# The modulation product of a decoder layer, feature tile by feature tile over four column groups

## The chip, the core and the metric

The kernel runs on one core of one Trainium2 chip. TensorE multiplies matrices into PSUM, VectorE (DVE), ScalarE (ACT) and GpSimd (POOL) work on rows of 128 partitions, and SyncE (SP) issues most of the DMAs. The engines run side by side, each its own instructions in a fixed order, and meet through semaphores. The metric is the device time in microseconds of one execution; of several runs the median counts.

## The reference

One decoder layer works on 1024 prompt tokens and on 8 sample sequences of 4 new tokens each, all of width 1024. Nine modulation vectors for each of nine conditions (the prompt's and eight samples') shift, scale and gate its three parts:

```python
mods = (silu(cond) @ ada_w + ada_b).reshape(B, 9, 1, 1024)
h = rms_norm(x, norm_ffn1) * (1 + mods[:, 1]) + mods[:, 0]
x = x + 0.5 * mods[:, 2] * swiglu_ffn(h, ffn1_wi, ffn1_wo)
h = rms_norm(x, norm_mix) * (1 + mods[:, 4]) + mods[:, 3]
...
x = x + mods[:, 5] * mix
h = rms_norm(x, norm_ffn2) * (1 + mods[:, 7]) + mods[:, 6]
x = x + 0.5 * mods[:, 8] * swiglu_ffn(h, ffn2_wi, ffn2_wo)
```

`mix` comes from a gated delta rule and from latent attention over a cache. `ada_w` is 1024 x 9216 in float32, 37.7 MB. The product with it has nine rows only, so nearly all of its work is to bring these weights past the array.

## The kernel before

The residual stream lies with features on partitions: three blocks (`xb`) of 352 token columns (1056 in all), each with 8 feature tiles of 128. The program is: load and transpose x, first norm, first FFN, mixer, second FFN. The order on each engine is set when the program is built, by a scheduler that simulates it; a few stretches of POOL are ordered by hand. On the chip every engine keeps that order.

**The modulation product** is the generator `ada(m0, nm, ...)` (L215). It makes `nm` vectors from number `m0` on, 1024 outputs each, cut into slices of 512. The conditions after silu (`cT`, padded to 32 columns, one tile per feature tile) are the stationary operand, the weights stream. Slice j accumulates in partitions 32j to 32j+31 of one PSUM bank (`acc`), which are columns 32j to 32j+31 of the array, a column group. The loops run slice by slice: for each j four loads (L225) of 256 features x 512 outputs (512 KB), and behind each load its two matmuls (L227) of 128 features; then a `yield`. So all eight feature tiles of one slice come before the next slice begins. At the end the rows are copied (`adarow`, L232), transposed (`adaT`, L235), and added to the bias (L239) into `modT`.

- Vectors 0 and 1 are made in the start (L1944), between the sums of the first norm and its application, with seven buffers of their own (`adaw` in the pool t0).
- Vector 2 alone, then 3 and 4, 5 and 6, 7 and 8 are made in the background of the first FFN (`background`, L1949). Their loads pass through the three buffers `wraw`, which the FFN's weights use too. The FFN calls `hook(us)` with a rough measure of the work done (L1959); for each PACE (1.85 for vector 2, then 8.0) the background goes on by one step, a load and its two matmuls.

**The FFN** (`ffn`, L345) takes 44 tiles of hidden features, two at a time. `up` makes gate and up products (`pg`), `down` the product with the second weights (`po`). Every weight tile is loaded into `wraw` (L106, L111), split by ACT (L97) and POOL or DVE (L100) into two float32r parts `whi` and `wlo`, and each product is three matmuls (`mm3`, L116 to L118) over 352 columns.

**SyncE** issues all these loads in one queue, in order: a load that waits for its buffer holds back what stands behind it.

Of the kernel before, what the change touches and what calls it, by code (L numbers as in the profile page):

```python
# [8 lines left out]
F32 = mybir.dt.float32  # L9
# [8 lines left out]
P = 128  # L18
# [16 lines left out]
# the projections of the mixer in turn: keys, queries, values and gates of GDN, latents and queries of MLA; from I on the  # L35
# triangular systems, from F on the norms of MLA's queries run beside
# [27 lines left out]
PACE = (1.85, 8.0)  # L64
# [6 lines left out]
class Banks:  # L71
    """PSUM pools by tag"""
# [8 lines left out]
class Kernel:  # L81
# [21 lines left out]
    def load_cols(self, w, c0, n):  # L103
        """n columns of w [1024, *] as a [128, 8, n] tile pair"""
        raw = self.wraw.tile([P, KT, P], F32, tag="wraw", name="wraw")
        self.nc.sync.dma_start(out=raw[:, :, :n], in_=w[:, c0:c0 + n].rearrange("(k p) c -> p k c", p=P))  # L106
        return raw
# [26 lines left out]
    def weights(self):  # L134
        """the pools that weights pass through, as a context"""
# [5 lines left out]
    def residents(self):  # L141
        """the residual stream, as a context"""
# [5 lines left out]
    def r(self, tp, shape, name, dt=F32):  # L148
        """a tile of the mixer's shared 1152-word slots"""
        return tp.tile(shape, dt, tag="r", name=name, bufs=RBUFS)  # L150

    def segs(self, c0, n):
        """token columns c0..c0+n as (block, column in block, length, offset)"""
# [8 lines left out]
    def tok_tiles(self):  # L162
        """(block, column, tokens, [(row, tokens, prompt?, first token)]) of the nine token tiles that no block edge cuts"""
# [11 lines left out]
    def load_x(self, ps, tag):  # L175
        """the residual stream, feature on the partition; the rows pass through the tiles of the first norm's results"""
# [16 lines left out]
    def small_vectors(self, tp, ps, tag):  # L193
        """ada_b (72 rows of 128) and the three norm gains (8 each), feature on the partition"""
# [20 lines left out]
    def ada(self, m0, nm, tp, ps, tag, bufs=0):  # L215
        """nm (1 or 2) modulation vectors from m0 on: silu(c) @ ada_w + ada_b, transposed; yields between loads"""
# [3 lines left out]
        for j in range(2 * nm):  # L220
            c0 = m0 * D + j * 512
            for kp in range(4):
                raw = (tp.tile([P, 2, 512], F32, tag="adaw", name="adaw", bufs=bufs) if bufs
                       else self.wraw.tile([P, 2, 512], F32, tag="wraw", name="adaw"))
                nc.sync.dma_start(out=raw, in_=w[kp * 256:(kp + 1) * 256, c0:c0 + 512].rearrange("(k p) c -> p k c", p=P))  # L225
                for k in range(2):
                    nc.tensor.matmul(acc[32 * j:32 * j + 32, :], self.cT[:, 2 * kp + k, :], raw[:, k, :],  # L227
                                     start=(kp == 0 and k == 0), stop=(kp == 3 and k == 1))
                yield
        row = tp.tile([P, 512], F32, tag="adarow", name="adarow", bufs=1)  # L230
        np_ = 64 * nm
        nc.scalar.copy(row[:np_], acc[:np_])  # L232
        pt = ps.tile([P, 4, 4, 32], F32, tag=tag, name="adaT")
        for q in range(4):
            nc.tensor.transpose(pt[:, q, :2 * nm, :].rearrange("p j r -> p (j r)"), row[:np_, q * P:(q + 1) * P], self.ident[:np_, :np_])  # L235
        bias = self.vecs[:, 0:72].rearrange("p (m k) -> p m k", k=KT)
        for j in range(2 * nm):
            m, k0 = m0 + j // 2, (j % 2) * 4
            nc.vector.tensor_tensor(out=self.modT[:, m, k0:k0 + 4, :], in0=pt[:, :, j, 0:NROW],  # L239
                                    in1=bias[:, m, k0:k0 + 4].unsqueeze(2).to_broadcast([P, 4, NROW]), op=ALU.add)  # L240
# [4 lines left out]
    def mod_finish(self, m):  # L245
        """scale rows become g * (1 + scale); the FFN gates are halved"""
# [9 lines left out]
    def norm(self, mscale, mshift, tp, ps, between=None):  # L256
        """between() is called where its work comes before the last of the norm's"""
# [8 lines left out]
    def norm_squares(self, b, tp, k=0, n=KT, eng=None):  # L266
        """the squares of features k..k+n of block b, added up"""
# [15 lines left out]
    def norm_sums(self, blocks, tp, ps):  # L283
        """the inverse roots of some blocks, a quarter of a block per column"""
# [13 lines left out]
    def norm_apply(self, b, mscale, mshift, tp, ps, turn=0):  # L298
        """the parts of block b, the first in the place of block b + turn"""
# [31 lines left out]
    def residual(self, b, d, m, ps, tp):  # L331
        """x += gate * ps for feature tile d of token block b"""
# [12 lines left out]
    def ffn(self, wi, wo, mgate, tp, ps, each, hook=lambda us: None, banks="B"):  # L345
        """each(b, d) follows when feature tile d of block b is complete"""
# [5 lines left out]
        def up(ffs):  # L352
            """some tiles of the hidden features, block by block"""
# [35 lines left out]
        for c in chunks:  # L389
            # the first tiles go together, as the norm of the later blocks is not there yet  # L390
# [10 lines left out]
    def store_y(self, ps, tag, block, halves):  # L401
        """the results of a block, or of halves of its features"""
# [52 lines left out]
    def proj_weights(self, eng=None):  # L455
        """the next tile of w_in's columns in the order of self.worder, as (hi, lo, columns)"""
# [15 lines left out]
    def proj(self, evac, ps, post=None):  # L472
        """the next tile of w_in's columns, transposed: evac(b, psum, rows); what follows from earlier tiles goes between its
# [1451 lines left out]
def body(tc, ins, outs):  # L1925
    k = Kernel(tc, ins, outs)
    nc = tc.nc
    with k.ctx:
        k.setup()
        k.dram()  # L1930
        def run(gen):
            for _ in gen:
                pass
# [87 lines left out]
```

## Time and profile before

| what | us |
| --- | --- |
| median of 3 runs (2957.89 to 2968.86) | 2967.14 |
| profiled execution, first to last instruction (span) | 2962.4 |
| start, up to the first matmul of the first FFN | 59.4 |
| first FFN, up to the mixer's first projection | 59.4 to 942.3 |
| mixer up to its output projection | 942.3 to 2087.9 |
| TensorE busy | 2824.4 |

For the profiled execution only the span is given; what lies around it is not shown apart.

How to read the profile: PE is TensorE's matmuls, PEld its weight loads, which overlap with them. A row of the timeline gives start, length, engine, line, operation, written tile <- read tiles, shape and count; rows of one kind that follow each other are merged, and the length reaches to the end of the last one, whose end is modelled. "[idle <-X]" is the time for which the engine stood still before, and what ended it. A matmul in float32 shows as two records. L12 is line 12 of the kernel; the lines of the changed kernel are shifted by a few.

### The profile page before, as it was taken

How to read it: one execution, taken by the hardware profiler on the slowest of the kernel's cores; microseconds unless marked ns; L12 is line 12 of the kernel's file. 1: busy time of each engine (PE TensorE's matmuls, PEld its weight loads, DVE VectorE, ACT ScalarE, POOL GpSimd, SP SyncE). 2: the span in 40 equal slices, each digit the busy share in tenths (PEclk: the TensorE clock that was granted, in tenths of full speed). 3: DMA queues.
4: the chain of work that ended last, by engine and by line, in shares of the span. 5: the costliest groups of instructions: out<-in, count | busy, mean ns of one | idle time of the engine just before them, and what ended most of it. 6: DMA issues, size and time to landing. Idle time of an engine off the chain costs nothing.

```text
span 2962.4 us, 45680 instructions
## 1 busy us (share of the span) xinstructions
PE 2824.4 (95%) x18596; PEld 2548.1 (86%) x18596; DVE 1579.8 (53%) x3258; ACT 919.0 (31%) x1674; POOL 801.9 (27%) x624
## 2 busy tenths in 40 slices
PE   7999999999998989889999988898899999999999
PEld 4788888899998889778887866675899999999998
DVE  5232322233337568997777677886463343333445
ACT  4211111111113453433676664443341111111111
POOL 3100011111113344445344456452221111111110
PEclk8999999999999999999999998997899999999999
DMA  7322233221113257344122234322301111111111
GB/s 234 108 86 79 86 100 93 76 67 43 43 39 101 69 159 194 121 142 148 33 58 60 58 68 129 87 62 48 120 29 58 43 50 51 43 43 44 57 36 59
DMA packets 295385, 238.76 MB, mean 81 GB/s; under 512 B 89390, under 2 KB 248870, under 8 KB 294408
## 3 DMA queue, kind: packets, MB, share of 16 engines
q1 hardware_dynamic: 285624, 207.54, 24.0%
q0 software_dynamic: 6144, 20.98, 2.2%
q10 hardware_dynamic: 3408, 7.33, 0.8%
q8 instruction: 146, 2.39, 0.3%
q14 instruction: 63, 0.52, 0.1%
HBM read 192.66 MB, written 43.15 MB: 80 GB/s over the span
## 4 chain that ended last, share of the span: by engine, by line
PE 41%; DVE 8%; issue 5%; POOL 4%; DMA 1%; ACT 1%; POOLq 0%; DVEq 0%; ACTq 0%
PE pg L116 6%; PE pg L118 6%; PE pg L117 6%; PE po L116 4%; PE po L117 4%; PE po L118 4%; POOL gt L1344 2%; PE kraw L116 1%; PE kraw L118 1%; PE kraw L117 1%; POOL gS L1344 1%; DVE cy L708 1%; DVE kss L1820 1%; PE pS L116 1%; DVE pv L522 1%
## 5 line engine op out<-in xcount | busy, mean ns | idle before, releaser
L116 PE MATMUL pg<-hhi,whi 128*128 128x352 f32 x2112 | 685.9, 325 | 1.9 <-ACT hhi L324 1.9
L118 PE MATMUL pg<-hhi,wlo 128*128 128x352 f32 x2112 | 680.9, 323 | 0.0
L117 PE MATMUL pg<-hlo,whi 128*128 128x352 f32 x2112 | 679.7, 322 | 0.5 <-POOL hlo L325 0.5
L336 DVE SCALAR_TENSOR_TENSOR x<-po,modT,x 128x352 f32<-128x352 f32 (+1 forms) x552 | 313.8, 572 | 573.3 <-PE po L118 566.1
L100 POOL TENSOR_TENSOR wlo<-wraw,whi 128x1024 fp32r<-128x1024 f32 x93 | 225.7, 2432 | 1422.7 <-ACT whi L97 1372.4
L116 PEld LDWEIGHTS pg<-hhi,whi 128*128 128x128 f32 x2112 | 396.9, 188 | 27.2 <-issue 18.4
L117 PEld LDWEIGHTS pg<-hlo,whi 128*128 128x128 f32 x2112 | 399.2, 189 | 3.3 <-issue 1.7
L118 PEld LDWEIGHTS pg<-hhi,wlo 128*128 128x128 f32 x2112 | 396.7, 188 | 5.9 <-issue 5.9
L116 PE MATMUL po<-ahl,whi 128*128 128x352 f32 x1056 | 344.2, 326 | 2.6 <-DVE rt L340 1.3
L117 PE MATMUL po<-ahl,whi 128*128 128x352 f32 x1056 | 339.9, 322 | 0.0
L118 PE MATMUL po<-ahl,wlo 128*128 128x352 f32 x1056 | 338.8, 321 | 0.0
L97 ACT CAST whi<-wraw 128x1024 fp32r<-128x1024 f32 x140 | 145.6, 1049 | 541.7 <-PE po L117 231.9
L366 DVE TENSOR_TENSOR fa<-fs,pg 128x352 f32<-128x352 f32 x132 | 68.4, 518 | 368.7 <-ACT fs L364 368.6
L364 ACT ACTIVATE fs<-pg 128x352 f32<-128x352 f32 x132 | 61.1, 463 | 581.4 <-PE pg L118 581.4
L1820 DVE TENSOR_REDUCE kss<-ksq 128x8 f32<-128x512 f32 x256 | 173.6, 681 | 80.5 <-ACT ksq L1819 78.3
L116 PEld LDWEIGHTS po<-ahl,whi 128*128 128x128 f32 x1056 | 198.0, 188 | 13.2 <-issue 8.9
L1819 ACT ACTIVATE ksq<-kraw 128x512 f32<-128x512 f32 x256 | 152.7, 599 | 156.7 <-PE kraw L118 120.5
L117 PEld LDWEIGHTS po<-ahl,whi 128*128 128x128 f32 x1056 | 200.0, 189 | 0.0
L118 PEld LDWEIGHTS po<-ahl,wlo 128*128 128x128 f32 x1056 | 198.5, 188 | 0.0
L116 PE MATMUL pp<-hhi,whi 128*128 128x352 f32 (+1 forms) x576 | 191.2, 333 | 5.7 <-ACT raw L689 2.4
L118 PE MATMUL pp<-hhi,wlo 128*128 128x352 f32 (+1 forms) x576 | 192.0, 335 | 2.9 <-POOL tss L719 2.1
L117 PE MATMUL pp<-hlo,whi 128*128 128x352 f32 (+1 forms) x576 | 190.6, 331 | 3.0 <-DVE hlo L328 2.0
(490 smaller groups left out, 4973.3 us busy)
## 6 DMA issues: line engine op xcount, KB each, us to landing
wraw<-ffn_wi SPq DMA_DIRECT2D x88, 512.0 KB
adaw<-ada_w SPq DMA_DIRECT2D x72, 512.0 KB
wraw<-ffn_wo SPq DMA_DIRECT2D x44, 512.0 KB
wraw<-w_in SPq DMA_DIRECT2D x23, 512.0 KB
x_d<-x SPq DMA_DIRECT2D x3, 1408.0 KB
x<-x_d SPq DMA_DIRECT2D x3, 1408.0 KB
dml<-dm_d SPq DMA_DIRECT2D x8, 512.0 KB
wraw<-w_out SPq DMA_DIRECT2D x8, 512.0 KB
```

The source lines that it names most:

```text
L97: nc.scalar.copy(hi, raw)
L100: eng.tensor_tensor(out=lo, in0=raw, in1=f(hi), op=ALU.subtract)
L116: nc.tensor.matmul(out, whi, ahi, start=first, stop=False)
L117: nc.tensor.matmul(out, whi, alo, start=False, stop=False)
L118: nc.tensor.matmul(out, wlo, ahi, start=False, stop=last)
L336: nc.vector.scalar_tensor_tensor(out=x[:, d, :n], in0=ps[:, :n], scalar=self.modT[:, m, d, 0:1], in1=x[:, d, :n], op0=ALU.mult, op1=ALU.add)
L364: nc.scalar.activation(s, pg[:, 0, :BW], AF.Silu)
L366: nc.vector.tensor_tensor(out=a, in0=s, in1=pg[:, 1, :BW], op=ALU.mult)
L522: nc.vector.tensor_tensor(out=t, in0=y, in1=y, op=ALU.mult)
L1344: mul = lambda out, a, b, op=ALU.mult: nc.gpsimd.tensor_tensor(out=out, in0=a, in1=b, op=op)
L1819: nc.scalar.activation(sq, kr, AF.Square)
L1820: nc.vector.tensor_reduce(out=ss[:, (j * 4 + m) * H:(j * 4 + m + 1) * H], in_=sq.rearrange("p (h d) -> p h d", h=H), axis=AX.X, op=ALU.add)
```

## The change

The four slices of two vectors (or of one vector, see below) advance together. A step loads two pieces of 128 features x 1024 outputs, 512 KB each, and issues four matmuls, one for each column group. For two vectors (`nm` = 2) the pieces are the same feature tile of both vectors, and there are eight steps. For one vector they are feature tiles s and s + 4 of that vector: column groups 0 and 1 sum up the first four feature tiles, groups 2 and 3 the last four, there are four steps, and the second pair of rows is added to the first after the transposes. `issue_after` puts the matmuls of groups 3, 0 and 1 behind that of group 2 on TensorE.

In the FFN the first piece of a step still goes through `wraw`; the second has one buffer of its own (`adaw`, bufs 1, in the pool tk). PACE is doubled, as a step now does the work of two. The rest of the diff takes out comments, and shifts the lines below.

```diff
--- before
+++ after
-PACE = (1.85, 8.0)
+PACE = (3.7, 16.0)
...
     def ada(self, m0, nm, tp, ps, tag, bufs=0):
...
         acc = ps.tile([P, 512], F32, tag=tag, name="ada")
-        for j in range(2 * nm):
-            c0 = m0 * D + j * 512
-            for kp in range(4):
-                raw = (tp.tile([P, 2, 512], F32, tag="adaw", name="adaw", bufs=bufs) if bufs
-                       else self.wraw.tile([P, 2, 512], F32, tag="wraw", name="adaw"))
-                nc.sync.dma_start(out=raw, in_=w[kp * 256:(kp + 1) * 256, c0:c0 + 512].rearrange("(k p) c -> p k c", p=P))
-                for k in range(2):
-                    nc.tensor.matmul(acc[32 * j:32 * j + 32, :], self.cT[:, 2 * kp + k, :], raw[:, k, :],
-                                     start=(kp == 0 and k == 0), stop=(kp == 3 and k == 1))
-                yield
+
+        def load(n, k, c0):
+            raw = (tp.tile([P, 1024], F32, tag="adaw", name="adaw", bufs=bufs or 1) if bufs or n
+                   else self.wraw.tile([P, 1024], F32, tag="wraw", name="adaw"))
+            nc.sync.dma_start(out=raw, in_=w[k * P:(k + 1) * P, c0:c0 + 1024])
+            return raw
+        nk = KT // (3 - nm)
+        for s in range(nk):
+            ks = (s, s) if nm == 2 else (s, s + nk)
+            raws = [load(n, k, m0 * D + (n * 1024 if nm == 2 else 0)) for n, k in enumerate(ks)]
+            def product(j):
+                return nc.tensor.matmul(acc[32 * j:32 * j + 32, :], self.cT[:, ks[j // 2], :], raws[j // 2][:, (j % 2) * 512:(j % 2) * 512 + 512],
+                                        start=(s == 0), stop=(s == nk - 1))
+
+            with self.tc.issue_after(product(2).ins):
+                for j in (3, 0, 1):
+                    product(j)
+            yield
         row = tp.tile([P, 512], F32, tag="adarow", name="adarow", bufs=1)
-        np_ = 64 * nm
-        nc.scalar.copy(row[:np_], acc[:np_])
+        nc.scalar.copy(row, acc)
         pt = ps.tile([P, 4, 4, 32], F32, tag=tag, name="adaT")
         for q in range(4):
-            nc.tensor.transpose(pt[:, q, :2 * nm, :].rearrange("p j r -> p (j r)"), row[:np_, q * P:(q + 1) * P], self.ident[:np_, :np_])
+            nc.tensor.transpose(pt[:, q].rearrange("p j r -> p (j r)"), row[:, q * P:(q + 1) * P], self.ident)
         bias = self.vecs[:, 0:72].rearrange("p (m k) -> p m k", k=KT)
-        for j in range(2 * nm):
-            m, k0 = m0 + j // 2, (j % 2) * 4
-            nc.vector.tensor_tensor(out=self.modT[:, m, k0:k0 + 4, :], in0=pt[:, :, j, 0:NROW],
-                                    in1=bias[:, m, k0:k0 + 4].unsqueeze(2).to_broadcast([P, 4, NROW]), op=ALU.add)
+        for j in range(4):
+            m, k0 = m0 + (j // 2 if nm == 2 else 0), (j % 2) * 4
+            v = self.modT[:, m, k0:k0 + 4, :]
+            nc.vector.tensor_tensor(out=v, in0=pt[:, :, j, 0:NROW],
+                                    in1=bias[:, m, k0:k0 + 4].unsqueeze(2).to_broadcast([P, 4, NROW]) if nm == 2 or j < 2 else v, op=ALU.add)
```

More of the change, by code (lines that the diff above doesn't have):

```diff
@@ L1943, in modulation @@
                             k.key_tables(tp, ps, "C")
-                            run(k.ada(0, 2, tp, ps, "C", 7))
+                            run(k.ada(0, 2, tp, ps, "C", 6))
                         k.load_x(ps, "C")
```

## The prediction, made before the changed kernel ran

> **What bounds the kernel now.** I read the page first, then the stages, then every place where L227, the modulation product, stands on TensorE. The page's line of busy times and its 40 slices say that TensorE is the bound except at the very start and in parts of the middle.
>
> ```profile
> PE 2824.4 (95%) x18596; PEld 2548.1 (86%) x18596; DVE 1579.8 (53%) x3258; ACT 919.0 (31%) x1674; POOL 801.9 (27%) x624
> PE   7999999999998989889999988898899999999999
> ```
>
> The second view gives busy time by stretch (start:end, length, then for each engine busy us and instructions; behind them the granted TensorE clock, the DMA share and GB/s). The rows are the first FFN with the background beside it (60 to 713 holds all of L227 that is left after the start), the stretch in which the mixer's work is mixed (1070 to 2088), and the second FFN.
>
> ```profile
> 60.00:713.00 653.00, 652.48 (x3597) 561.63 (x3597) 205.18 (x437) 109.43 (x179) 84.50 (x42) 0.99 0.27 81
> 1070.00:2088.00 1018.00, 916.42 (x7258) 771.90 (x7256) 787.27 (x1619) 510.19 (x1006) 474.64 (x433) 0.94 0.36 99
> 2185.00:2962.40 777.40, 770.61 (x4844) 767.52 (x4842) 334.40 (x657) 144.25 (x232) 110.09 (x51) 1.00 0.15 48
> ```
>
> In the first FFN TensorE idles 0.5 us of 653, the clock is full, and no other engine is busy for a third of the time. What is taken from TensorE there comes off the end one for one. The second FFN is the same work without a modulation product beside it: 777 us with TensorE still 99% busy, so the other engines keep that pace. The first takes 942.3 - 59.4 = 883, by the timeline's rows for its first matmul and the mixer's:
>
> ```profile
> 59.42 0.59 PE L116 MATMUL pg<-hhi,whi 128*128 128x352 f32 x2 [1.87 <-ACT hhi L324]
> ...
> 942.28 0.52 PE L116 MATMUL pp<-hhi,whi 128*48 128x352 f32 x2 [0.91 <-ACT hhi L324]
> ```
>
> The view by stretch for L227 alone shows what stands to be taken:
>
> ```profile
> 28.00:60.00 32.00, 25.05 (x64) 6.05 (x64) 0.93 0.80 262
> 60.00:713.00 653.00, 103.61 (x224) 20.24 (x224) 0.99 0.27 81
> ```
>
> The 288 records are 144 matmuls, so each float32 matmul leaves two. 64 records stand in the start, 224 in the FFN.
>
> **The FFN's part, before.** The timeline (start, length with the last one's tail, line, count) around one visit of the product among the FFN's matmuls, and around two longer visits:
>
> ```profile
> 112.37 0.32 PE L118 MATMUL pg<-hhi,wlo 128*128 128x352 f32 x1
> 112.63 1.90 PE L227 MATMUL ada<-adaw,cT 128*32 128x512 f32 x4
> 114.46 0.43 PE L116 MATMUL pg<-hhi,whi 128*128 128x352 f32 x1
> 114.73 0.32 PE L117 MATMUL pg<-hlo,whi 128*128 128x352 f32 x1
> 114.89 0.32 PE L118 MATMUL pg<-hhi,wlo 128*128 128x352 f32 x1
> ...
> 162.94 3.65 PE L227 MATMUL ada<-adaw,cT 128*32 128x512 f32 x12
> ...
> 330.14 5.34 PE L227 MATMUL ada<-adaw,cT 128*32 128x512 f32 x12
> ```
>
> Matmuls of the FFN start 0.16 us apart (114.73, 114.89). From the start at 112.37 to that at 114.73 there are 2.36 us where two steps of 0.16 would do: the visit costs 2.04 us. In the run at 330.14 twelve records start within 5.34 less one tail of 0.59, so they are (5.34 - 0.59) / 11 = 0.43 us apart. Four of those are 1.72; the other 0.32 us is what going to the narrow shape and back costs (0.31 with unrounded starts). Between these two rows the timeline has 49 visits:
>
> ```profile
> 68.02 1.04 PE L227 MATMUL ada<-adaw,cT 128*32 128x512 f32 x2
> ...
> 596.88 1.90 PE L227 MATMUL ada<-adaw,cT 128*32 128x512 f32 x4
> ```
>
> 224 x 0.43 + 49 x 0.31 = 111.5 us. The run at 162.94 is 1.69 us shorter than its twin at 330.14, which is four records: there the end of one slice met the start of the next, in another column group, and their records ran side by side. That makes 109.8 us, and the two FFNs differ by 883 - 777 = 106.
>
> **Four side by side.** The trace has one line that already feeds four column groups in turn, the product of exponentials and latents (L1702, float32, 32 output rows each, 128 columns wide):
>
> ```profile
> 1737.34 1.95 PE L1702 MATMUL psc<-ck,pr 128*32 128x128 f32 x64
> ```
>
> By width one such record takes 0.43 / 4 = 0.107 us. One after the other 64 would take 6.9 us; four at a time they take 16 x 0.107 = 1.7 plus a tail, and 1.95 is what stands there. So four groups run at four times the rate, with four different moving operands. That a 512 wide product does the same is seen for two groups only (162.94).
>
> The order on TensorE at one visit in the first FFN (adaw is a loaded piece of the weights, ada the accumulator; each row x2 is two matmuls), before:
>
> ```order
> L118 MATMUL po_1210<-ahl_740,wlo_1199 128x352
> L227 MATMUL ada_786<-adaw_1218,cT_64 32x512 x2
> L227 MATMUL ada_786<-adaw_1294,cT_64 32x512 x2
> L227 MATMUL ada_786<-adaw_1382,cT_64 32x512 x2
> L116 MATMUL po_1222<-ahl_668,whi_1192 128x352
> ```
>
> and at the corresponding place of the changed kernel:
>
> ```order
> L118 MATMUL po_1212<-ahl_740,wlo_1201 128x352
> L232 MATMUL ada_819<-adaw_1238,cT_64 32x512 x2
> L232 MATMUL ada_819<-adaw_1236,cT_64 32x512 x2
> L116 MATMUL pg_1448<-hhi0_442,whi_1438 128x352
> ```
>
> The two rows of the changed kernel are the four column groups of one step. Counted through its whole order, the 28 steps in the first FFN make 33 visits: 24 whole, and four steps torn into two or three pieces. A visit then costs two records after each other, 0.86, some 0.02 for starts that are not quite together, and 0.31 for the change of shape: 1.19 us, whether it holds one matmul or four. 33 x 1.19 = 39.3. **The FFN gains 109.8 - 39.3 = 70.5 us.** Bounds from the nearest rows: only two at a time, as at 162.94, gives 28 x 4 x 0.43 + 33 x 0.31 = 58.4 and a gain of 51; the change of shape at nothing gives 28 x 0.88 and a gain of 85. I take 70.5, for L1702 shows both the four and the same change of shape.
>
> The Trainium skill, page "TensorE: Matmul & The Clock Gate", section "Measured speedup vs the span model", states 2.38 times for three column tiles of 512 and 3.07 times for four row tiles, less than the trace's four. By 3.07 a whole step would take 8 x 0.43 / 3.07 = 1.12 instead of 0.88 us, and the gain would be 28 x 0.24 = 6.7 us less; no row here shows four groups at 512.
>
> **The start.** There 25.05 us of product stand between the first norm's sums and its end, on the path:
>
> ```profile
> 28.34 9.17 PE L227 MATMUL ada<-adaw,cT 128*32 128x512 f32 x20 [0.34 <-DVE idx L437]
> 38.78 7.08 PE L227 MATMUL ada<-adaw,cT 128*32 128x512 f32 x20
> 46.24 8.80 PE L227 MATMUL ada<-adaw,cT 128*32 128x512 f32 x24
> 55.72 0.66 PE L235 MATMUL adaT<-ident,adarow 128*128 128x128 f32 x4 [0.68 <-ACT adarow L232]
> ```
>
> Eight steps of 0.88 would be 7 us, 18 less, but the weights are not there so soon:
>
> ```profile
> 32.00:36.00 4.00, 4.00 (x10) 0.91 (x10) 2.23 (x4) 2.23 (x3) 1.69 (x1) 0.93 0.90 241
> 48.00:52.00 4.00, 4.00 (x15) 1.18 (x14) 0.00 (x0) 0.00 (x0) 0.00 (x0) 1.00 1.05 388
> 52.00:56.00 4.00, 3.32 (x11) 0.83 (x9) 0.00 (x0) 0.90 (x2) 0.00 (x0) 1.00 0.20 74
> 56.00:60.00 4.00, 1.75 (x14) 1.15 (x12) 3.43 (x11) 3.26 (x7) 0.56 (x1) 0.98 0.02 3
> 60.00:64.00 4.00, 3.48 (x13) 3.46 (x13) 4.00 (x7) 3.36 (x8) 3.19 (x4) 0.50 0.00 0
> ```
>
> The DMA runs at its full share up to 52 us plus 4 x 74 / 388 = 0.8. The queue of SyncE before, behind the fourth FFN weight (wraw_597):
>
> ```order
> L225 DMA adaw_397<-ada_w 128x2x512
> L225 DMA adaw_632<-ada_w 128x2x512
> L225 DMA adaw_401<-ada_w 128x2x512
> L225 DMA adaw_405<-ada_w 128x2x512
> L225 DMA adaw_409<-ada_w 128x2x512
> L225 DMA adaw_413<-ada_w 128x2x512
> L225 DMA adaw_417<-ada_w 128x2x512
> L225 DMA adaw_421<-ada_w 128x2x512
> L225 DMA adaw_636<-ada_w 128x2x512
> L225 DMA adaw_671<-ada_w 128x2x512
> ```
>
> and now, behind the same weight (632, 671 and 704 belong to the next vector):
>
> ```order
> L225 DMA adaw_403<-ada_w 128x1024
> L225 DMA adaw_632<-ada_w 128x1024
> L225 DMA adaw_409<-ada_w 128x1024
> L225 DMA adaw_671<-ada_w 128x1024
> L225 DMA adaw_411<-ada_w 128x1024
> L225 DMA adaw_417<-ada_w 128x1024
> L225 DMA adaw_419<-ada_w 128x1024
> L225 DMA adaw_704<-ada_w 128x1024
> ```
>
> Before, two foreign loads followed the last own one, 0.52 MB each, 1.35 us at 388 GB/s: the last own one (421) landed near 52.8 - 2.7 = 50.1, and TensorE was done with it at 55.0. Now two foreign loads stand ahead of the last own one (419) instead of one: 1.35 us later, less about 0.5 for the pause at 32 to 36 (share 0.90), which earlier freed buffers fill: about 51.0. One step more, 0.9 to 1.7 us by clock, ends at 51.9 to 52.7. **The start gains 2.7 us**, its cover being the DMA; bounds 0 and 18. The Trainium skill, the page named above, section "What's actually happening", has the array fall to half its clock after an idle window of some 3.4 us; the row at 60 to 64 (0.50 behind a stretch with 1.75 of 4 us busy) agrees, and by it the last step takes the 1.7. What follows, norm and first FFN matmuls, moves up unchanged; it ran at half clock at 60 to 64 already.
>
> **Costed at nothing.** Two more adds on VectorE, a 128 row copy on ScalarE and full transposes for the one vector alone lie beside TensorE's work in the FFN. DMA volume is the same. The order in the mixer between 1070 and 2088 comes out differently, with the same instructions: nothing on average, though TensorE idles 102 us there and its clock is 0.94, so a reshuffle has room both ways; I allow 15 us, an estimate: a tenth of that idle time and lost clock (0.06 x 1018 = 61).
>
> **Sum.** 70.5 + 2.7 = 73.2. The span would fall from 2962.4 to 2889.2. The median of the runs shown is 2967.1, 4.7 above the span; less 73.2 it is **2894 us**.
>
> **Rivals.** (a) Two at a time: as above the FFN gains 51, the start 2: 2914. Speaks for it: at 512 wide the trace shows two only. Against: L1702.
> (b) The four do not overlap at all: 28 x 8 x 0.43 + 33 x 0.31 = 106.6 against 109.8, and no gain at the start: 2964. Both rows above speak against it.
> (c) The mixer's new order costs or gives over 20 us: 2915 to 2945, or under 2872.
> (d) Slower: each step's second piece has a single buffer, so its load is issued only when the step before is through, and SyncE's FFN weights wait behind it. A load on idle queues:
>
> ```profile
> 71.23 2.72 SPq L225 DMA_DIRECT2D adaw<-ada_w  x2
> ...
> 72.00:73.00 1.00, 1.00 (x5) 0.43 (x4) 1.00 (x3) 0.97 (x3) 0.42 (x1) 1.00 0.72 78
> 73.00:74.00 1.00, 1.00 (x5) 0.52 (x4) 1.00 (x3) 0.84 (x2) 0.64 (x1) 1.00 0.90 338
> 74.00:75.00 1.00, 1.00 (x8) 1.00 (x7) 1.00 (x3) 0.75 (x2) 0.50 (x1) 1.00 0.65 139
> ```
>
> Issued at 71.23, its 0.52 MB are through near 74.5: 3.3 us. Were it exposed at all 28 steps, it would cost 92 us: 2986. It decides from 73.2 / 28 = 2.6 us of wait per step. Against it: the closest steps in the new order have 30 matmuls between them, 30 x 0.16 = 4.8 us, which leaves 1.5 to spare; it would take other waits in SyncE's queue ahead of the load.
>
> **Chances and range.** The forecast (2872 to 2913) 0.78; (c) 0.05 up and 0.05 down; (a) 0.05; (b) 0.03; (d) 0.04. The range 2872 to 2916 takes in the forecast, (a) and the mixer's 15 us. Faster by over 0.5% (15 us, about what a measurement of this kernel can tell from no change): 0.93; within: 0.03; slower: 0.04.
>
> **What would show it.** The product's busy time in the first FFN falls from 103.6 to about 35 us; its visits read x8 and last about 1.1 us; the mixer's first projection starts some 73 us earlier. Two at a time would read 1.9 us per x8. In the start TensorE waits for adaw, and its last product ends near 52. Rival (d) shows as waits of TensorE for adaw or whi beyond 60 us. A mixer stretch longer or shorter than 1018 us by over 15 makes the sum wrong.

## The result and the profile after

The changed kernel takes **2893.0 us** (median of 5 runs, 2880.28 to 2896.78) where the kernel before takes 2967.14 (2957.89 to 2968.86, now of 5 runs): a ratio of 0.975, 95% interval 0.9726 to 0.9774, so 74.1 us less, where 73.2 were predicted. Two more measurements of the same changed kernel follow among the experiments: 2900.46 and 2894.56.

The profiled execution was the fastest of the five (2880.28, span 2878.3). Its page's busy line and the slices of TensorE and of its clock:

```profile
PE 2745.4 (95%) x18596; PEld 2527.9 (88%) x18596; DVE 1586.6 (55%) x3260; ACT 916.9 (32%) x1674; POOL 803.8 (28%) x624
...
PE   6999999999999898889999988888999999999999
...
PEclk7999999999999999989999999997999999999999
```

TensorE has the same 18596 instructions and is busy 79 us less. The view by stretch shows where: the first FFN with the background beside it, the whole first FFN, the mixed part of the mixer (up to its output projection), the second FFN; then the modulation product's line (now L232) alone, in the start and in the first FFN.

```profile
60.00:713.00 653.00, 653.00 (x4054) 618.01 (x4053) 237.26 (x497) 122.69 (x200) 93.69 (x45) 1.00 0.28 85
57.90:868.40 810.50, 807.13 (x5001) 769.28 (x5001) 308.92 (x658) 156.53 (x251) 126.91 (x67) 1.00 0.27 81
996.80:2005.40 1008.60, 918.50 (x7257) 770.36 (x7255) 785.06 (x1618) 508.10 (x1003) 475.51 (x433) 0.94 0.35 99
2101.70:2878.30 776.60, 769.78 (x4841) 766.61 (x4839) 334.12 (x657) 144.19 (x232) 109.60 (x51) 1.00 0.15 48
```

```profile
28.00:60.00 32.00, 13.89 (x64) 1.60 (x60) 0.55 0.77 267
60.00:713.00 653.00, 35.04 (x224) 5.07 (x224) 1.00 0.28 85
```

In the window from 60 to 713 us TensorE is busy all 653 us, and more FFN matmuls fit into it (4054 records, 3597 before). The product's own time there fell from 103.61 to 35.04 us. The first FFN took 883 us and takes 810.4; the second is unchanged (777). One visit of the product on TensorE's timeline:

```profile
276.55 0.32 PE L118 MATMUL pg<-hhi,wlo 128*128 128x352 f32 x1
276.80 1.07 PE L232 MATMUL ada<-adaw,cT 128*32 128x512 f32 x8
277.80 0.43 PE L116 MATMUL pg<-hhi,whi 128*128 128x352 f32 x1
278.06 0.32 PE L117 MATMUL pg<-hlo,whi 128*128 128x352 f32 x1
```

Eight records end within 1.07 us; from the FFN's last start before them (276.55) to the second behind them (278.06) are 1.51 us, less two steps of 0.16 that would stand there anyway: 1.19 us for a visit. The first FFN has 33 visits, and none of them has idle time before it. Its first two:

```profile
64.80 1.06 PE L232 MATMUL ada<-adaw,cT 128*32 128x512 f32 x6
66.95 1.05 PE L232 MATMUL ada<-adaw,cT 128*32 128x512 f32 x2
```

They are one torn step: two records cost a visit (1.17 us) as much as eight (1.19).

One line of the change is missing from the diff shown above: in the start, `run(k.ada(0, 2, tp, ps, "C", 7))` became `run(k.ada(0, 2, tp, ps, "C", 6))`, so six buffers hold the start's loads instead of seven. The seventh load therefore waits for the first step, which an experiment below takes up.

### The profile page after: what moved, and what is told of

Same layout as the page of the kernel before. It is cut to its first block, busy times and chain, and to the rows that moved or that the text cites. A ratio compares the mean times of both kernels' runs of the same rounds, so it can differ in the third digit from the quotient of the medians.

```text
span 2878.3 us, 45708 instructions
## 1 busy us (share of the span) xinstructions
PE 2745.4 (95%) x18596; PEld 2527.9 (88%) x18596; DVE 1586.6 (55%) x3260; ACT 916.9 (32%) x1674; POOL 803.8 (28%) x624
## 4 chain that ended last, share of the span: by engine, by line
PE 43%; DVE 7%; issue 5%; POOL 4%; DMA 2%; ACT 1%; POOLq 0%; DVEq 0%; ACTq 0%; SPq 0%
PE pg L116 6%; PE pg L118 6%; PE pg L117 6%; PE po L116 4%; PE po L117 4%; PE po L118 4%; POOL gt L1353 2%; PE kraw L116 1%; PE kraw L118 1%; PE kraw L117 1%; POOL gS L1353 1%; PE pS L116 1%; DVE kss L1829 1%; PE pS L117 1%; PE pS L118 1%
```

## Experiments

Each edit is against the changed kernel. Stage lengths are read from TensorE's timeline: the first FFN runs from its first matmul to the mixer's first projection.

### One column group at a time

The change's steps, two loads and four matmuls each, and its turns; but the four matmuls of a step are four feature tiles of one slice, in one column group. With that the loads have the old shape again (256 features x 512 outputs, still 512 KB), and the copies and transposes at the end are the old ones.

```diff
-            nc.sync.dma_start(out=raw, in_=w[k * P:(k + 1) * P, c0:c0 + 1024])
+            nc.sync.dma_start(out=raw.rearrange("p (k c) -> p k c", k=2), in_=w[k * 256:(k + 1) * 256, c0:c0 + 512].rearrange("(k p) c -> p k c", p=P))
...
-        nk = KT // (3 - nm)
-        for s in range(nk):
-            ks = (s, s) if nm == 2 else (s, s + nk)
+        steps = [(j, kq) for j in range(2 * nm) for kq in range(2)]
+        for j, kq in steps:
...
-                return nc.tensor.matmul(acc[32 * j:32 * j + 32, :], self.cT[:, ks[j // 2], :], raws[j // 2][:, (j % 2) * 512:(j % 2) * 512 + 512],
+                return nc.tensor.matmul(acc[32 * j:32 * j + 32, :], self.cT[:, 4 * kq + k, :], raws[k // 2][:, (k % 2) * 512:(k % 2) * 512 + 512],
```

> Undoes the column groups alone: the step of the change (two loads, four matmuls, doubled PACE, the second load's own buffer) stays, but the four matmuls of a step belong to one slice and so to one column group, slice by slice as before. The order has 35 visits in the first FFN. Theory (side by side is what counts): 224 records at 0.43 us and 35 visits at 0.31 us, 107 us on top of the FFN's own work of 771 us (810.4 less 33 x 1.19): the first FFN takes 878 us, the kernel 2960 us, within 0.5% of before. Rival (fewer and longer visits or the loads' shape are what counts): the first FFN stays near 810 us, the kernel near 2893.

Measured: 2969.86 us, ratio 0.9991 (0.9973 to 1.0008). A whole step on the timeline:

```profile
123.16 0.32 PE L118 MATMUL pg<-hhi,wlo 128*128 128x352 f32 x1
123.42 3.62 PE L233 MATMUL ada<-adaw,cT 128*32 128x512 f32 x8
126.97 0.43 PE L116 MATMUL pg<-hhi,whi 128*128 128x352 f32 x1
...
62.20:936.10 873.90, 97.63 (x224) 20.70 (x224) 2.34 (x4) 1.00 0.25 75
```

The last row is the product's line over the first FFN. The same eight records that take 1.07 us side by side take 3.62 us in one column group. Fewer and longer visits gave 9 us in the first FFN (873.9 against 882.9), some of it where the end of one slice met the next; the other 63.5 us of the gain come with the column groups. This kernel undoes the loads' shape as well, so it does not part the two; the next one does, for it keeps the new loads.

### Two column groups at a time

One load and the two matmuls that read it make a step, and PACE is the old one.

```diff
-PACE = (3.7, 16.0)
+PACE = (1.85, 8.0)
...
-        for s in range(nk):
-            ks = (s, s) if nm == 2 else (s, s + nk)
-            raws = [load(n, k, m0 * D + (n * 1024 if nm == 2 else 0)) for n, k in enumerate(ks)]
+        for s, n in ((s, n) for s in range(nk) for n in range(2)):
+            k = s if nm == 2 else s + n * nk
+            raw = load(0, k, m0 * D + (n * 1024 if nm == 2 else 0))
...
-            with self.tc.issue_after(product(2).ins):
-                for j in (3, 0, 1):
-                    product(j)
+            with self.tc.issue_after(product(2 * n).ins):
+                product(2 * n + 1)
```

> Two column groups at a time: a step is one load of 128 features x 1024 outputs and its two matmuls, with the PACE of before and all loads of the FFN through wraw. 48 visits in the first FFN, between one and six matmuls each. Theory: a visit costs 0.31 us and every round of records 0.43 us, some 110 to 120 rounds: 62 to 67 us on top of 771, a first FFN of 833 to 838 us and a kernel of 2916 to 2921 us. Rival (the gain is not the rounds but the number of visits, 49 before, 48 here, 33 in the change): the first FFN near 880 us and the kernel near 2965.

Measured: 2922.1 us, ratio 0.982 (0.9788 to 0.9852), and a first FFN of 835.8 us. A step (first row), and the product's line over the first FFN:

```profile
103.10 1.05 PE L233 MATMUL ada<-adaw,cT 128*32 128x512 f32 x4
...
57.90:893.70 835.80, 54.77 (x224) 8.14 (x224) 2.35 (x4) 1.00 0.26 79
```

Two groups side by side take as long (1.05 us) as four do (1.07), and as one matmul alone does: the price belongs to the visit. The total lies 1 us above the range expected, the first FFN inside it. Here are 48 visits (43 of about 1.18 us, five with three steps and 2.03 us), 61.0 us in all where the change's 33 cost 39.3, and the first FFN is 25 us longer.

### The start without most of its loads

Steps 3 to 7 of the start multiply the pieces of step 2 again: ten of its sixteen loads, and with them the right values of the first two vectors, are left out.

```diff
-            raws = [load(n, k, m0 * D + (n * 1024 if nm == 2 else 0)) for n, k in enumerate(ks)]
+            if bufs and s >= 3:
+                raws = kept
+            else:
+                raws = kept = [load(n, k, m0 * D + (n * 1024 if nm == 2 else 0)) for n, k in enumerate(ks)]
```

> Leaves out the last ten of the sixteen weight loads of vectors 0 and 1 in the start; the matmuls read the third step's pieces again (so the modulation is not the reference's). Theory (the start is bound by the weights' arrival): without them TensorE does not wait for adaw any more, the last product ends by 37 us and the first FFN matmul moves from 57.9 to between 40 and 46 us, behind the norm's roots and its application. Rival (something else on the way, the norm or the half clock, sets the start): it stays within 2 us of 57.9. The first FFN stays at 810 us in both.

Measured in one execution: the first matmul of the first FFN at 47.33 us instead of 57.94, 1.3 us later than the range expected.

```profile
37.66 1.88 PE L235 MATMUL ada<-adaw,cT 128*32 128x512 f32 x10
42.58 0.85 PE L317 MATMUL rb<-ident,nr 88*128 88x88 f32 x4 [3.04 <-DVE nr L536]
...
47.33 0.96 PE L116 MATMUL pg<-hhi,whi 128*128 128x352 f32 x2 [1.54 <-ACT hhi L336]
```

The product is through at 39.5 us (37 were expected), where with all loads it is through at 53.1: the start was bound by the arrival of the weights. What comes next there is 3.04 us of wait for the first norm's inverse roots on DVE. The total (2899.46, one run) shows nothing of the 10 us, since the mixed part of this execution's mixer took 1034.6 us, 26 more than in the change's profile, at a lower granted clock; the two kernels measured again, below, come back to that.

### Whole steps as closed blocks

The four matmuls of a step are scheduled as one unit that nothing is put into, with seven buffers in the start: 28 visits, none torn.

```diff
-            with self.tc.issue_after(product(2).ins):
-                for j in (3, 0, 1):
+            with self.tc.tile_critical():
+                for j in (2, 3, 0, 1):
...
-                            run(k.ada(0, 2, tp, ps, "C", 6))
+                            run(k.ada(0, 2, tp, ps, "C", 7))
```

> The change with two edits: the four matmuls of a step are scheduled as one block, so that none of the 28 steps in the first FFN is torn (28 visits instead of 33), and the start has seven weight buffers again instead of six. Theory: five visits at 1.19 us less, a first FFN of 771.1 + 28 x 1.19 = 804.4 us instead of 810.4; in the start the seventh load is issued near 20 us instead of 29.8, the pause of the DMA at 28 to 32 shrinks, and the first FFN starts 1 to 2 us before 57.9. In all 6 to 8 us less than the change in a run of the same clock. Rival (a torn step costs nothing, as its matmuls are the same in number): 810 us.

A miss: 2932.84 us, ratio 0.9896 (0.9869 to 0.9922), 40 us slower than the change. The first FFN takes 828.0 us instead of the 804 expected, and the start ends at 88.4 us. A visit, and three places in the start:

```profile
288.03 0.32 PE L116 MATMUL pg<-hhi,whi 128*128 128x352 f32 x1
288.90 1.07 PE L232 MATMUL ada<-adaw,cT 128*32 128x512 f32 x8 [0.55 <-issue]
290.08 0.42 PE L116 MATMUL po<-ahl,whi 128*128 128x352 f32 x1
290.34 0.32 PE L117 MATMUL po<-ahl,whi 128*128 128x352 f32 x1
```

```profile
34.75 1.94 PE L232 MATMUL ada<-adaw,cT 128*32 128x512 f32 x8 [6.39 <-DMA wraw<-ffn_wi]
...
67.94 1.94 PE L232 MATMUL ada<-adaw,cT 128*32 128x512 f32 x8 [7.26 <-DMA adaw<-ada_w]
74.80 1.93 PE L232 MATMUL ada<-adaw,cT 128*32 128x512 f32 x8 [4.93 <-DMA adaw<-ada_w]
```

The product itself is as short as before (1.07 us), but TensorE stands idle 0.43 to 0.56 us ahead of 26 of the 28 blocks (1.23 and 1.49 ahead of two) and 0.11 behind most: as if the block waited until what stands before it is through. That reading is not shown; for 23 of the blocks the profile names nothing that they wait for. This visit costs 1.99 us (from 288.03 to 290.34, less 0.32); the 28 cost 1.96 on average, 54.8 us where 33 open ones cost 39.3. In the start the blocks wait for loads in turn, up to 7.26 us each.

### Two steps in one closed block

Eight matmuls, two for each group, in one block for each visit, with two buffers for the second pieces: 14 visits. The start has two steps a visit too, and seven buffers.

```diff
-PACE = (3.7, 16.0)
+PACE = (7.4, 32.0)
...
-        for s in range(nk):
+        for s0 in range(0, nk, 2):
+            todo = []
+            for s in (s0, s0 + 1):
+                for n in range(2):
+                    k = s if nm == 2 else s + n * nk
+                    todo.append((s, n, k, load(n, k, m0 * D + (n * 1024 if nm == 2 else 0))))
...
+            with self.tc.tile_critical():
+                for t in (1, 0, 3, 2):
+                    for h in range(2):
+                        product(*todo[t], h)
```

> Two steps of the change at one visit (four loads, eight matmuls as one block, PACE doubled once more, two buffers for the second pieces, seven in the start). 14 visits in the first FFN. Theory: 14 x (4 x 0.43 + 0.04 + 0.31) = 29 us instead of 39.3, a first FFN of 800 us, if four loads in the 32 units of PACE arrive in time; the kernel some 10 to 12 us below the change in a run of the same clock. Rival (two steps bring twice the loads at once into the buffers that the FFN's weights share, and TensorE waits for adaw or whi): waits of TensorE in the first FFN, and 810 us or more.

A miss again: 2924.09 us, ratio 0.9863 (0.9839 to 0.9888), a first FFN of 814.6 us where 800 were expected, and a start up to 79.2 us. The idle time around a block is the same (0.43 to 0.53 us ahead of 12 of the 14, 0.11 behind), and two blocks wait longer, for a weight of the FFN:

```profile
395.68 1.92 PE L237 MATMUL ada<-adaw,cT 128*32 128x512 f32 x16 [2.04 <-DMA wraw<-ffn_wi]
```

That is the rival's sign, but both such waits together are 3.4 us. A visit costs 2.93 us on average, where eight matmuls that stay open cost 2.05 (below). Halving the visits did not make up for closing them.

### The two kernels again

The changed kernel and the kernel before, unedited, each profiled again. The first row of each pair below is the first FFN, the second the mixed part of the mixer.

> The changed kernel once more, for a second profile. The first profile's stretch from the first transpose of the mixer to its output projection took 1008.6 us, 8.6 less than before, with TensorE at half clock for 133 us of it (before 144). Theory (chance of the clock, not the new order): this profile has a stretch between 1015 and 1035 us with more time at half clock, and the first FFN again 810.4. Rival (the new order of the mixer is worth 8.6 us): 1007 to 1011 us again.

> The kernel before once more, for a second profile. Theory (chance of the clock): its stretch from the first transpose of the mixer to the output projection is not again 1017.2, but moves by several us with the time at half clock. Rival: 1017 us again within 2. The first FFN is 882.9 again, within 1, in both.

Measured: the changed kernel 2900.46 us (2895.64 to 2902.7, ratio 0.9776, 0.9755 to 0.9798), the kernel before 2971.16 in one run. The changed kernel:

```profile
59.70:871.20 811.50, 808.15 (x5001) 770.31 (x5001) 308.84 (x658) 156.46 (x251) 126.82 (x67) 1.00 0.27 81
1001.20:2026.50 1025.30, 934.81 (x7256) 782.73 (x7253) 784.04 (x1618) 509.36 (x1003) 475.53 (x433) 0.92 0.35 97
```

and the kernel before:

```profile
59.90:941.30 881.40, 877.66 (x5001) 784.16 (x5002) 303.30 (x658) 155.37 (x249) 126.83 (x67) 1.00 0.25 75
1071.00:2094.50 1023.50, 922.78 (x7256) 776.43 (x7254) 789.30 (x1619) 509.35 (x1003) 473.31 (x433) 0.93 0.35 99
```

The first FFN repeats within 1.5 us (810.4 and 811.5; 882.9 and 881.4). The mixer does not: the changed kernel's own two profiles differ by 16.7 us there (1008.6 and 1025.3), and TensorE's busy time by 16.3 (918.50 and 934.81) with the same instructions, at a granted clock of 0.94 and 0.92. So the 8.6 us that the mixer seemed to gain in the first profile need no new order: the clock of one execution moves it by more.

### Two steps a visit, left open; and seven buffers in the start

Two kernels. In the first, a visit has eight matmuls as above, in the start too and with seven buffers there, but they are placed by priority behind the first one instead of being closed into a block.

```diff
+            first = product(*todo[3], 0)
+            with self.tc.high_priority(), self.tc.issue_after(first.ins):
+                for t, h in ((3, 1), (2, 0), (2, 1), (1, 0), (1, 1), (0, 0), (0, 1)):
+                    product(*todo[t], h)
```

> The changed kernel with two steps in one visit (eight products, two for each column group, two buffers for the second pieces, PACE 7.4 and 32, seven buffers in the start), the products placed by priority and by an order behind the first one, not as one closed block as in the two-step kernel before. Theory (the price of a visit is the change of shape plus two records for each two rounds of four groups, and what the closed block lost came from closing it): in the first FFN 10 visits of x16 (1.72 + 0.31 + 0.02 = 2.05 us each), 4 of x12 and 4 of x4 (the torn ones, about 1.7 and 0.9 to 1.2 us), 33 to 34 us in all where the change had 39.3: the first FFN 804 to 806 us against 810 to 812. The start ends within 2 us of the change's 57.9 to 59.7. Total 5 to 7 us below the change's, about 2886 to 2895 by the clock's chance in the mixer. Rival 1 (a visit's closing costs, not the block, made the two-step kernel slow: two pieces wait for each other's loads): TensorE shows waits for adaw in the FFN, and the first FFN takes 812 to 816. Rival 2 (the visit's cost is in its records alone, the change of shape is hidden): the first FFN stays at 810 to 812.

Measured: a first FFN of 806.5 us, half a us above the theory's 804 to 806 and 4 to 5 us below the change. A visit:

```profile
275.97 0.32 PE L118 MATMUL pg<-hhi,wlo 128*128 128x352 f32 x1
276.21 1.92 PE L237 MATMUL ada<-adaw,cT 128*32 128x512 f32 x16
278.07 0.43 PE L116 MATMUL pg<-hhi,whi 128*128 128x352 f32 x1
278.33 0.32 PE L117 MATMUL pg<-hlo,whi 128*128 128x352 f32 x1
```

From 275.97 to 278.33 less 0.32 are 2.04 us, two rounds for one change of shape, and nothing idle. So it was the closing of the block that cost. The total misses what was expected: 2899.7 us (ratio 0.9767, 0.9748 to 0.9785) is not below the change's. The start took as long, and the mixer 1026.6 us at a clock of 0.92.

The second kernel is the change with seven buffers in the start, its only edit the 6 turned back into 7.

> The changed kernel with seven instead of six buffers for the start's loads, nothing else. Theory (the start is bound by the weights' arrival, and the pause of the DMA near 28 to 32 us, where the seventh load waits for a buffer, costs about what is lacking to its full share): the start's last own load lands 0.3 to 1.0 us earlier, and the first matmul of the first FFN comes at 57.0 to 59.0 where the change's two profiles had 57.9 and 59.7; the first FFN 810 to 812 as in the change; total within 3 us of the change's at the same clock. Rival (TensorE's own pace binds the start): no movement of the start at all, the last product waits less for its load.

Measured: 2894.7 us (ratio 0.9735, 0.971 to 0.976). The first FFN matmul comes at 57.87 us where the change's two profiles so far had 57.94 and 59.65. The DMA's share and GB/s (last two columns) from 28 to 32 us, in the changed kernel and then in this one:

```profile
28.00:32.00 4.00, 4.00 (x28) 1.30 (x28) 3.69 (x6) 2.96 (x4) 2.21 (x2) 0.66 0.94 233
```

```profile
28.00:32.00 4.00, 3.66 (x18) 0.99 (x18) 3.25 (x5) 2.62 (x4) 3.49 (x3) 0.50 1.15 300
```

The pause is filled, and from the first product to the transposes (`adaT`) are 24.8 us instead of 25.9 and 26.4. The two profiles of the next section agree: 24.9 us with seven buffers, 25.5 with six. The missing buffer costs about 1 us.

### Both together, beside the change

Single steps and seven buffers in the start, two steps a visit in the FFN, and the changed kernel once more on the same chip.

```diff
+        W = 1 if bufs else 2
+        for s0 in range(0, nk, W):
+            todo = []
+            for s in range(s0, s0 + W):
```

> Single steps in the start with seven buffers (as in the seven-buffer run), two steps a visit in the first FFN (as in the open two-step run). Theory: the parts add up. First matmul of the first FFN as in the seven-buffer run (57 to 59, 24.8 us from the first product to adaT), the first FFN 805 to 807, so 5 to 6 us below the change at the same clock; total 2885 to 2895, the change run beside it 2889 to 2901. Rival: what the visits save in the first FFN is given back behind it (another order in the mixer): the mixer's length less half of its half-clock time is 942 or more instead of 938 to 942, and the total is that of the change.

> The changed kernel once more, unchanged, beside the run before it on the same chip. Theory: the first FFN 810 to 812, first matmul of it 57.5 to 60, total 2889 to 2901, and 5 to 6 us above the run beside it at the same clock. Rival (no difference): medians within 2 us of each other.

"Half-clock time" is summed from the trace's records of the granted clock, from the mixer's first projection to the last record, 2 to 3 us behind the last instruction; so some of it lies outside the mixed part. Taking half of it off a length estimates what that length would be at full clock. Measured: both together 2886.6 us (2885.93 to 2894.57; ratio to before 0.9744, 0.9726 to 0.9762), the change 2894.56 (2887.27 to 2900.59; 0.9758, 0.9737 to 0.9778). The first FFN of the one and then of the other, and the change's mixer:

```profile
58.70:865.20 806.50, 803.18 (x5000) 772.83 (x5000) 303.37 (x658) 156.09 (x251) 127.14 (x67) 1.00 0.26 81
```

```profile
58.50:869.80 811.30, 807.98 (x5000) 770.13 (x5000) 309.22 (x658) 156.32 (x251) 126.52 (x67) 1.00 0.27 81
999.60:2021.80 1022.20, 924.87 (x7255) 775.24 (x7253) 785.60 (x1618) 508.05 (x1002) 474.48 (x433) 0.93 0.35 98
```

The first FFN is 4.8 us shorter, as in the run with two steps a visit, and the start is no worse (58.7 and 58.5 us). The medians differ by 8 us, more than the FFN explains; the mixer took 1013.9 us here and 1022.2 in the change's profile, with half-clock times of 144.2 and 160.4. Less half of that time the mixers are 941.8 and 942.0 us (949.0 and 948.8 with the half-clock time of the mixed part alone), so nothing was given back there. The 4.8 us of the first FFN are shown; that the whole kernel is faster than the change is likely, but the two intervals overlap.

## Why the prediction was right

**The first FFN's term held.** Predicted were 109.8 - 39.3 = 70.5 us; the lengths of the first FFN give 882.2 (mean of 882.9 and 881.4) less 811.1 (of 810.4, 811.5 and 811.3), 71.1 us. Each factor stands as costed: 33 visits, 1.19 us each. The one step that no row of before showed, four groups at a width of 512, came out as L1702 had suggested: eight records start within 0.48 us, where one column group needs 3.03 (3.62 less a tail of 0.59). That the visits set the first FFN's length is shown by taking their sum (each from start to start, as above) off it, kernel by kernel; what is left stays within 4 us while the sums differ by 76:

| kernel | visits | their sum, us | first FFN, us | difference |
| --- | --- | --- | --- | --- |
| before | 49 | 109.8 | 882.9 | 773.1 |
| one column group | 35 | 102.2 | 873.9 | 771.7 |
| two column groups | 48 | 61.0 | 835.8 | 774.8 |
| the change | 33 | 39.3 | 810.4 | 771.1 |
| whole steps as closed blocks | 28 | 54.8 | 828.0 | 773.2 |
| two steps in one closed block | 14 | 41.0 | 814.6 | 773.6 |
| two steps a visit, open | 18 | 33.4 | 806.5 | 773.1 |

The last row's sum is 10 visits of 2.05, 4 of 2.04 and 4 of 1.18 us; for the kernel before it is 109.7 when the visits are summed one by one.

The Trainium skill's page "TensorE: Matmul & The Clock Gate", section "Measured speedup vs the span model", gives 2.38 times for three column tiles and 3.07 for four row tiles of 512. It has no figure for four column groups, and this trace's is higher: 8 records of 0.43 us each, 3.44, pass in 0.88 us, 3.9 times, so the 6.7 us which the 3.07 would have taken off the gain were not lost.

**The start's term was over-sized.** Predicted were 2.7 us, from the last product's end at about 52.3 instead of 55.0. The first FFN matmul came at 57.9, 59.7 and 58.5 us in three profiles of the change, and at 59.4 and 59.9 before: 1 us earlier on average. Counted from the first product, which itself moves by up to 1.8 us from execution to execution, the change's three are 30.1, 30.1 and 29.6, before's two 31.1 and 31.4: 1.3 us. The bound was named rightly, and its place too:

```profile
48.62 1.93 PE L232 MATMUL ada<-adaw,cT 128*32 128x512 f32 x8 [3.19 <-DMA adaw<-ada_w]
51.13 1.94 PE L232 MATMUL ada<-adaw,cT 128*32 128x512 f32 x8 [0.58 <-DMA adaw<-ada_w]
53.77 1.12 PE L243 MATMUL adaT<-ident,adarow 128*128 128x128 f32 x4 [0.70 <-ACT adarow L240]
54.68 1.71 PE L314 MATMUL rb<-ident,nr 88*128 88x88 f32 x8
57.94 0.95 PE L116 MATMUL pg<-hhi,whi 128*128 128x352 f32 x2 [1.54 <-ACT hhi L333]
...
48.00:52.00 4.00, 2.80 (x14) 0.40 (x16) 0.00 (x0) 0.00 (x0) 0.00 (x0) 0.50 0.67 267
52.00:56.00 4.00, 3.19 (x19) 1.89 (x12) 0.92 (x6) 0.58 (x1) 0.00 (x0) 0.50 0.07 6
```

The last own load released TensorE at 51.1 us here, where 51.0 was worked out, but that is luck: this execution began its product 0.5 us earlier than before's. Counted from the first product, the three profiles of the change have this release at 23.3, 23.7 and 22.8 us, where 51.0 would be 22.7. Three terms of the start were off.

- "... less about 0.5 for the pause at 32 to 36 (share 0.90), which earlier freed buffers fill": with one buffer fewer the pause stays. The release comes 0.6 us late on average; in the two kernels that differ from the change's start by the seventh buffer alone it comes at 22.2 and 22.4 us.
- "One step more, 0.9 to 1.7 us by clock": it took 1.94 us in all three profiles, 0.6 more than the middle of that range.
- "What follows, norm and first FFN matmuls, moves up unchanged; it ran at half clock at 60 to 64 already": before, the transposes and the rest up to 60 us ran at full clock, and the row from 60 to 64 with its 0.50 comes behind them. Now in two of three profiles the transposes took 1.1 us where they took 0.66, and from these to the first FFN matmul it is 4.2 us instead of 3.7. In the third the clock was back for them, and it is 3.7 as before; on average what follows took 0.3 us more:

```profile
53.30 1.94 PE L232 MATMUL ada<-adaw,cT 128*32 128x512 f32 x8 [0.58 <-DMA adaw<-ada_w]
55.95 0.66 PE L243 MATMUL adaT<-ident,adarow 128*128 128x128 f32 x4 [0.71 <-ACT adarow L240]
...
59.65 0.95 PE L116 MATMUL pg<-hhi,whi 128*128 128x352 f32 x2 [1.88 <-ACT hhi L333]
```

So of the 1.4 us that are lacking, some 0.6 are the missing buffer's, and the rest comes with the half clock. In the first profile that lasts from 34 to 61 us, although no single wait of TensorE in it is over 3.2 us; an idle window of some 3.4 us, with which the prediction reckons, is not needed (the last section counts this).

**The mixer's order** was put at nothing with 15 us either way. The first profile was 8.6 us shorter, the repeats 8.1 and 5.0 longer than the 1017.2 before, and less half of its half-clock time the mixer took 942.2, 938.0 and 942.0 us with the change (half-clock times 132.8, 174.7, 160.4) and 945.1 and 942.0 without (144.2, 163.0). By this estimate the order is worth about 3 us, too little to tell from none while three executions of one kernel differ by 4; what moves the total by some 15 us is the clock.

**The rivals.** Two at a time (2914) is refuted by the visit's 1.07 us for x8; a kernel that does take two at a time lands at 2922.1. The rival's 58.4 us for the visits stand beside 61.0 measured; the other 5 us lie within what the mixer moves (1027.8 us in that kernel's profile). No overlap at all (2964) is what one column group gives: 2969.86. The late loads (2986) would have shown as idle time of TensorE in the FFN; from 60 to 713 us it is busy 653.00 of 653.00.

**The sum** of 73.2 beside 74.1 between the medians is nearer than its parts deserve, and so partly luck: 71 and 1 us are what the stages show, and the rest is within what the clock of the mixer moves. The two repeats had 2900.46 and 2894.56, 66 and 73 us below the medians of before beside them (2966.62 and 2967.3).

## What to carry to other kernels

Here a product with few output rows cost a visit of the array, not its matmuls: fill the four column groups with independent work at each visit, and price the visit (change of shape plus the longest column group), then count visits in the order of the program. Where a small job is bound by its loads, speeding its arithmetic only makes the engine idle, and what comes behind it may run at half clock; look at the granted clock of the next stage before crediting it as unchanged. Judge changes of a few us by the length of the stage they touch, not by the total.

## What the runs showed of the hardware

- The mixer's length follows the granted clock from one execution of the same program to the next: 1008.6, 1025.3 and 1022.2 us with 0.94, 0.92 and 0.93. Its half-clock time was 132.8, 174.7 and 160.4 us. Over all thirteen profiles the half-clock time inside the mixer (first to output projection) goes from 125 to 182 us, and the mixer's length from 1137 to 1164.
- In every trace the granted clock changes only on a grid of 3.413 us: its stretches at one value last 6.83, 10.24, 3.41, 27.31 us at the start of the change's first profile. The grid lies differently in each execution, its first line 0.6 to 3.4 us behind the first instruction. The Trainium skill, in "TensorE: Matmul & The Clock Gate", section "What's actually happening", has the clock set over windows that run freely and do not begin with the kernel; these records agree. Whether the place in a window at which the mixer begins decides its clock stays open, for no run held it fixed. But the three executions (before, the change, closed blocks) that began it 1.4 to 2.7 us into a window had 125 to 134 us of half clock in it; the other ten, which began it less than 0.7 us from a window's edge, had 136.5 to 182.
- A window (3.413 us, from one line of that grid to the next) need not be idle to cost the clock. Counted over the thirteen traces, none of the 208 half-clock windows with TensorE busy for less than 70% was followed by one at full clock, and none of the 147 full-clock windows busy for less than 40% either. The start of the change is at half clock from 34 to 61 us in windows that are 32 to 79% busy, and is released behind one of 95%.
- Closing eight records into one scheduled block left TensorE idle 0.43 us or more ahead of it and 0.11 behind, mostly with no wait that the profile names; the same records left open had no idle time.
- Loads with rows of 4 KB (1024 outputs) moved 396 to 415 GB/s from 44 to 48 us in the change's three profiles and the two kernels with seven buffers and single steps there; those of 2 KB moved 387 to 393 in before's two profiles and the kernel with one column group, at about the same full share. From 40 to 44 us the former varied from 357 to 405. What else lay on the queues was not held fixed, so the rows' length as the cause is not shown. The change's first profile:

```profile
44.00:48.00 4.00, 1.43 (x8) 0.00 (x0) 0.51 (x1) 0.00 (x0) 0.00 (x0) 0.50 1.02 409
```
